# Six split-weight places instead of four, one product order for all paired projections, and seven-product gqk, gv and gr in a hybrid decoder layer

## The chip, the cores and the metric

The kernel runs on one core of one Trainium2 chip, in one launch. The metric is the device time of one execution in microseconds; lower is better. Nothing is shared between cores: there are no collectives. All inputs lie in HBM as float32, already cut by the host into tiles of 128 rows by 512 columns.

## The reference

One decoder layer on 256 tokens of width 2048, all in float32. The tokens are normalised and multiplied by one wide combined projection. Its slices feed three mixers, whose outputs are projected back, gated, added and projected once more. A gated feed-forward network follows.

```
h = rmsnorm(x, attn_norm)
proj = h @ w_in
(gq, gk, gv, gr, ga1, sq, sk, sv, mq, gates) = split(proj)
log_a = log_sigmoid(ga1 @ gla_w_a2 + gla_b_a) / 16
o_gla = rmsnorm(gla_mixer(gq, gk, gv, log_a)) ; y_gla = (o_gla * silu(gr)) @ w_br_gla
y_sb  = stick_breaking_mixer(rmsnorm(sq), rmsnorm(sk), sv) @ w_br_sb
y_mem = memory_mixer(rmsnorm(mq), m_k, m_v) @ w_br_mem       # m_k, m_v from rmsnorm(mem) @ w_mem_kv
merged = g0 * y_gla + g1 * y_sb + g2 * y_mem                  # g = sigmoid(gates)
x = x + merged @ w_o
gate, up = split(rmsnorm(x, ffn_norm) @ w_gate_up)
x = x + (silu(gate) * up) @ w_down
```

Widths: gq and gk are 512 each, gv, gr, sq, sk, sv and mq 1024 each, the three gates 2048 each, the feed-forward inner width is 5632. The linear attention (gla) has four heads with a state of 128 by 256 that is carried over chunks of 64 tokens; stick-breaking attention has eight heads of 128; the memory attention has four heads of 256 over 256 memory tokens.

## The kernel before

**Split products.** TensorE works here on a rounded float32 type, so each operand is split into a high part (rounded by ScalarE, `ACT`) and a low part (the difference, by VectorE, `DVE`). Each product of a 128x128 activation block with a 128x512 weight block is three matmuls: high by high, high by low, low by high. Activations are split once and kept. Weights are split as they come from HBM: `split` (lines 134 to 141) casts on ACT (line 137) and subtracts on DVE (line 138), 128 by 1024 elements at a time, which is two blocks of the contraction.

**Two kinds of places.** A *raw place* holds four weight blocks as loaded (1 MB); `loads` (line 161) takes one from the list `free_raw`, and its `done` gives it back. A *split place* holds the high and low part of two blocks; `parts` (line 166) walks round the list `splits`. `widen` (line 90) adds places of both kinds. Up to line 956 there are three raw and four split places of the pool `ring1`. Between lines 608 and 696 two more raw places lie in `opool`, in whatever outputs of 128x8x256 do not use yet, and up to line 748 one more in `pre`. From line 956 on `ring2` adds three raw places and one split place, and in the feed-forward part `ring3` adds one split place.

**Plain product.** `gemm` (line 183) makes one output block of 512 columns for both halves of 128 tokens: 16 contraction blocks by 2 halves by 3 matmuls are 96 matmuls. `project` (line 475) calls it twice for a width of 1024.

**Seven products.** `sgemm` (line 216) makes a pair of column blocks (j = 0, 1) for both token halves (t = 0, 1). Over 2p contraction blocks it multiplies a two by two block matrix by seven products instead of eight (Strassen's scheme in Winograd's form); the other contraction blocks are done plainly by `rest`. The products are `p1` to `p3`, `q4`, `p5` to `p7`, named a, b, e, f, g, h, i in the order list at lines 354 to 362. Products take 3p matmuls each and one split place for two blocks; a `rest` step takes 12 matmuls and one split place. The activation sums (`sx`, `sm_`, `sf`, `sd`) are made in advance by `make_forms`. The weight sums are made in the raw places: 21 += 22 in g and 21 += 12 in h by DVE (line 263), 22 += 12 by an accumulating DMA from the POOL queue (line 325). The sum 11 += 21 is made by DVE before f, or, where `moved` is set, by a second accumulating DMA in `p2` (line 305). `put` copies the first product from a `tmp` tile into an output in PSUM (line 288), and the later ones by DVE (line 290). PSUM has four `acc` and four `tmp` tiles; an `sgemm` uses four and two.

**The order list.** There are four orders: `late` (the activation sums are still being made), `moved`, p equal to 4 without `moved`, and p equal to 2. The instructions pass through a scheduler that lays out each engine's stream ahead of time by priority and its own cost estimates, so neighbours can change places; each engine then runs its stream in order.

**Background work.** `step`, called after each split, advances one piece of work from the list `background`: attention chunks, transposes, norms. `flush` runs all that is left.

**Stages around the change.** Plain: memory keys and values and mq, until about 142 us. Seven products with p = 4 through `wide` (line 672): sq, sk, sv, until about 293 us; the memory attention is background of sq, and it splits its outputs into `o_mem` at once (line 670). Plain: gqk and gv (lines 744 and 745, until about 396 us) with stick-breaking attention as background, which splits its outputs into `o_sb` (line 739). Then `pre` is released, the narrow decay projection `w_ga` runs (lines 751 to 766), then gr, plain (lines 899 to 908), with its sigmoid made of exponentials and a logarithm. The linear attention `gla` (line 789) is background once the first block of gr is issued. Then the memory branch: four times a plain gate block and a plain branch block, until about 604 us. Then seven products for the gates of the other two branches (`w_gate`, line 968, p = 4, not `moved`), with plain branch products between; then `w_o` (line 998, p = 2; the first call `late`); then the feed-forward part from about 951 us: eleven `w_gate_up` calls (line 1029, the first p = 2 and `late`, ten p = 4 and `moved`), five `w_down` calls (line 1067, p = 4, not `moved`), and two plain blocks at the end.

## Time and profile before

| What | Value |
|---|---|
| Median of 3 runs | 1646.2 us (1645.76 to 1649.24) |
| Profiled execution, its own time | 1647.21 us |
| Profiled execution, its span | 1645.4 us |
| Granted TensorE clock, mean over the span | 0.999 |
| Busy: TensorE, VectorE, ScalarE, GpSimd | 99%, 78%, 60%, 3% |
| Instructions on TensorE | 7314 matmuls, 7314 weight loads |
| Bytes moved by DMA | 368.82 MB |

The span goes from the first to the last instruction; the profiled execution's own time is 1.8 us longer, and 1.0 us above the median of the runs. A matmul's row shows its whole passage through the array, about 0.39 us for 512 columns; matmuls follow each other much closer than that, so what one costs has to be read from the distance between starts. "Idle" in a row is the time in which the engine did nothing just before the instruction, and behind the arrow stands what ended the wait.

### The profile page before, as it was taken

The page shows a single profiled execution, that of the slowest core. Times are in us where ns is not written, and L with a number is a line of the kernel's source. Part 1 is how long each engine was busy: PE and PEld are TensorE (multiplying, and loading weights), DVE is VectorE, ACT ScalarE, POOL GpSimd, SP SyncE. Part 2 cuts the span into 40 slices and gives each one's busy share as a digit, 9 for nine tenths or more (in the row PEclk, how much of TensorE's full clock was granted, in tenths as well). Part 3 has the DMA queues.
Part 4 walks back from the last instruction along what each step waited for, and adds up shares of the span by engine and source line. Part 5 has one row for each costly group of instructions (what it writes and reads, how often), then busy time and mean ns, then how long its engine had stood idle before and what let it go on. Part 6 is the DMA issues. An engine that isn't in the chain of part 4 may idle for free.

```text
span 1645.4 us, 19330 instructions
## 1 busy us (share of the span) xinstructions
PE 1629.8 (99%) x7314; PEld 1334.9 (81%) x7314; DVE 1291.2 (78%) x1491; ACT 988.0 (60%) x1204; POOL 53.8 (3%) x70
## 2 busy tenths in 40 slices
PE   8999999999999999999999999999999999999998
PEld 6888787888877878888888888888888888888887
DVE  6857788764565667887897798988888998888994
ACT  7755666654644556556555666666666666666662
POOL 0000000000000000000000000000110000110000
PEclk9999999999999999999999999999999999999999
DMA  8784575544544467667556758686897686897692
GB/s 327 280 325 125 189 249 158 200 161 156 183 154 154 157 228 284 191 215 255 174 210 220 254 181 259 216 298 234 258 274 255 193 302 240 257 271 253 193 343 89
DMA packets 59406, 368.82 MB, mean 224 GB/s; under 512 B 6544, under 2 KB 11152, under 8 KB 16688
## 3 DMA queue, kind: packets, MB, share of 16 engines
q1 hardware_dynamic: 49968, 320.17, 53.4%
q0 software_dynamic: 8704, 46.67, 14.2%
q8 instruction: 57, 0.93, 0.2%
q10 hardware_dynamic: 640, 0.75, 0.1%
q14 instruction: 37, 0.30, 0.1%
HBM read 320.89 MB, written 8.39 MB: 200 GB/s over the span
## 4 chain that ended last, share of the span: by engine, by line
PE 96%; DVE 1%; DMA 1%; ACT 1%; issue 0%; ACTq 0%; DVEq 0%
PE acc L250 15%; PE acc L251 15%; PE acc L248 15%; PE acc L209 10%; PE acc L210 10%; PE acc L211 10%; PE tmp L250 5%; PE tmp L251 5%; PE tmp L248 5%; PE tmp L431 2%; DVE wl L138 1%; ACT wh L137 1%; DMA raw<-in_w_gate_up 1%; DMA raw<-in_w_mem_kv 0%; PE tmp L635 0%; PE tmp L863 0%
## 5 line engine op out<-in xcount | busy, mean ns | idle before, releaser
L138 DVE TENSOR_TENSOR wl<-raw,wh 128x1024 fp32r<-128x1024 f32 (+1 forms) x728 | 876.9, 1220 | 278.4 <-ACT wh L137 267.4
L137 ACT CAST wh<-raw 128x1024 fp32r<-128x1024 f32 (+1 forms) x728 | 753.9, 1051 | 536.1 <-PE acc L211 212.9
L251 PE MATMUL acc<-wh,hl 128*128 128x512 f32 x452 | 175.9, 389 | 0.0
L250 PE MATMUL acc<-wl,hh 128*128 128x512 f32 x452 | 175.9, 389 | 0.0
L248 PE MATMUL acc<-wh,hh 128*128 128x512 f32 x452 | 175.8, 390 | 0.0
L209 PE MATMUL acc<-wh,xTh 128*128 128x512 f32 x384 | 152.7, 398 | 0.0
L211 PE MATMUL acc<-wh,xTl 128*128 128x512 f32 x384 | 149.9, 390 | 0.0
L210 PE MATMUL acc<-wl,xTh 128*128 128x512 f32 x384 | 149.8, 390 | 0.0
L263 DVE TENSOR_TENSOR raw<-raw 128x1024 f32<-128x1024 f32 x115 | 139.7, 1221 | 4.5 <-DMA raw<-in_w_gate_up 3.0
L209 PE MATMUL acc<-wh,oh 128*128 128x512 f32 x320 | 125.2, 393 | 2.6 <-ACT wh L137 1.6
L210 PE MATMUL acc<-wl,oh 128*128 128x512 f32 x320 | 124.9, 390 | 1.1 <-DVE wl L138 1.1
L211 PE MATMUL acc<-wh,ol 128*128 128x512 f32 x320 | 124.8, 390 | 0.0
L248 PE MATMUL acc<-wh,xTh 128*128 128x512 f32 x280 | 110.1, 395 | 1.3 <-ACT wh L137 1.3
L250 PE MATMUL acc<-wl,xTh 128*128 128x512 f32 x280 | 109.7, 392 | 0.5 <-DVE wl L138 0.5
L251 PE MATMUL acc<-wh,xTl 128*128 128x512 f32 x280 | 109.4, 391 | 0.0
L250 PEld LDWEIGHTS acc<-wl,hh 128*128 128x128 f32 x452 | 84.9, 188 | 17.7
L248 PEld LDWEIGHTS acc<-wh,hh 128*128 128x128 f32 x452 | 84.7, 188 | 17.8 <-ACT wh L137 0.2
L251 PEld LDWEIGHTS acc<-wh,hl 128*128 128x128 f32 x452 | 84.8, 188 | 17.6
L248 PE MATMUL tmp<-wh,sh 128*128 128x512 f32 x222 | 89.4, 403 | 1.8 <-ACT wh L137 1.7
L250 PE MATMUL tmp<-wl,sh 128*128 128x512 f32 x222 | 87.3, 393 | 0.7 <-DVE wl L138 0.7
L251 PE MATMUL tmp<-wh,sl 128*128 128x512 f32 x222 | 87.6, 395 | 0.0
L209 PEld LDWEIGHTS acc<-wh,xTh 128*128 128x128 f32 x384 | 72.2, 188 | 16.4 <-issue 2.2
(297 smaller groups left out, 2497.1 us busy)
## 6 DMA issues: line engine op xcount, KB each, us to landing
raw<-in_w_gate_up SPq DMA_DIRECT2D x88, 1024.0 KB, 5.9
raw<-in_w_in SPq DMA_DIRECT2D x72, 1024.0 KB, 4.9
raw<-in_w_down SPq DMA_DIRECT2D x44, 1024.0 KB, 6.5
raw<-raw POOLq DMA_DIRECT2D x35, 1024.0 KB, 7.9
raw<-in_w_gate SPq DMA_DIRECT2D x32, 1024.0 KB, 4.9
raw<-in_w_o SPq DMA_DIRECT2D x16, 1024.0 KB, 5.0
raw<-in_w_mem_kv SPq DMA_DIRECT2D x15, 1024.0 KB, 5.4
raw<-in_w_br_mem SPq DMA_DIRECT2D x8, 1024.0 KB, 5.2
```

What stands on the lines that cost most here:

```text
L137: act.copy(hi, src)
L138: dve.tensor_tensor(lo, src, hi.bitcast(F32), op=ALU.subtract)
L209: pe.matmul(o[t][:], xh[:, s], wh[:, j], start=k == 0, stop=False)
L210: pe.matmul(o[t][:], xh[:, s], wl[:, j], start=False, stop=False)
L211: pe.matmul(o[t][:], xl[:, s], wh[:, j], start=False, stop=k == nk - 1)
L248: pe.matmul(dst[:], xh, wh, start=id(dst) not in begun, stop=False, skip_group_check=True)
L250: pe.matmul(dst[:], xh, wl, start=False, stop=False, skip_group_check=True)
L251: pe.matmul(dst[:], xl, wh, start=False, stop=last, skip_group_check=True)
L263: dve.tensor_tensor(x, x, y, op=ALU.add)
L431: pe.transpose(dst, src, ident)
```

## The change

The change has five parts.

- **Places.** The raw places in `opool` are given up. `opool` gets one tag `o` with four places of equal size; the outputs use them, and two entries of `splits` point to them, so weights are split into six places instead of four, from line 608 on. One entry is taken back after gr and the other when `ring2` opens. `ring2` gets two raw and two split places instead of three and one. So raw places go from six to four in mq, sq, sk and sv, stay at four in gqk and gv, are four instead of three in gr, and five instead of six from `w_gate` to the end; split places go from four to six up to gr, to five in the memory branch, and later from five to six, and from six to seven in the feed-forward part.
- **Outputs split late.** `o_mem` and `o_sb` are first kept whole as float32, copied by ACT alone, and split later by `split_later` as background work: `o_mem` just before the memory branch, `o_sb` at the start of `w_gate`.
- **One order.** All calls but the `late` ones use one order, in which two steps of `rest` come between a and g, p7 follows p6, and p2 follows p7. `moved` is the default, so `w_gate` and the second `w_o` call make 11 += 21 by DMA; `late` calls never do, and `w_down` still uses DVE.
- **gqk, gv and gr by seven products**: gqk and gv with p = 2, gr with p = 4.
- **Order of stages.** gr stands before `w_ga`, with nothing in the background; `gla` becomes background of the memory branch alone.

```diff
-        splits.extend([(pool, w)] * w)
+        splits.extend([(pool, None, w)] * w)
...
-        pool, n = splits[turn[0] % len(splits)]
+        pool, tag, n = splits[turn[0] % len(splits)]
+        if tag:
+            both = pool.tile([P, 2, IT], F32R, tag=tag, name="w", bufs=n)
+            return [both[:, i] for i in range(2)]
...
-    def sgemm(xs, forms, w, blks, p, row0=0, late=False, moved=False):
+    def sgemm(xs, forms, w, blks, p, row0=0, late=False, moved=True):
...
-            if moved:
+            if moved and not late:
                 nc.gpsimd.dma_start(q[11][0][:, :p], q[21][0][:, :p], accum_op=ALU.add)
...
-            prod(o[1, 0], single(0, 1), 11, last, *([] if moved else [(11, 21)]))
+            prod(o[1, 0], single(0, 1), 11, last, *([] if moved and not late else [(11, 21)]))
...
-        elif moved:
-            seq = [a, g, *r0[:2], h, *r0[2:], b, e, *r1[:2], i, *r1[2:3], f, *r1[3:]]
-        elif p == SP:
-            seq = [a, g, *r0[:2], h, *r0[2:], e, *r1[:2], i, b, *r1[2:3], f, *r1[3:]]
         else:
-            seq = [a, *l21, g, *r0[:2], h, *r0[2:], e, *l12, *r1[:1], i, *l22, b, *l11, *r1[1:3], f, *r1[3:]]
+            seq = [a, *l21, *r0[:2], g, *r0[2:], h, *l22, i, b, *l11, *r1[:2], e, *l12, *r1[2:3], f, *r1[3:]]
...
-        return [opool.tile([P, 8, T], F32R, tag=f"o{x}", name=f"o{x}") for x in "hl"]
+        return [opool.tile([P, 8, T], F32R, tag="o", name=f"o{x}", bufs=4) for x in "hl"]
...
-    free_raw.extend([(pre, "raw", 1), (opool, "oh", 2), (opool, "ol", 2)])
+    free_raw.append((pre, "raw", 1))
+    splits.extend([(opool, "o", 4)] * 2)
...
-    o_mem = outT()
+    def whole():
+        return opool.tile([P, 8, T], F32, tag="o", name="o", bufs=4)
+
+    def split_later(o):
+        high, low = outT()
+
+        def work():
+            for c in range(0, 8, 4):
+                split(high[:, c : c + 4], low[:, c : c + 4], o[:, c : c + 4])
+                yield
+
+        background.append(work())
+        return high, low
+
+    o_mem = whole()
...
-        split(*(x[:, 2 * h : 2 * h + 2].rearrange("p c t -> p (c t)") for x in o_mem), o[:])
+        act.copy(o_mem[:, 2 * h : 2 * h + 2].rearrange("p c t -> p (c t)"), o[:])
...
-    def wide(dst, c0):
-        for j, result in sgemm(xs, sx, w_in, (c0 // NB, c0 // NB + 1), SP, moved=True):
+    def wide(dst, c0, p=SP):
+        for j, result in sgemm(xs, sx, w_in, (c0 // NB, c0 // NB + 1), p):
...
-        split(o_sb[0][:, h], o_sb[1][:, h], o[:, :T])
+        act.copy(o_sb[:, h], o[:, :T])
...
-    project(gqk, xs, w_in, O_GQ, r_x)
-    project(gv, xs, w_in, O_GV, r_x)
+    wide(gqk, O_GQ, 2)
+    wide(gv, O_GV, 2)
+    flush()
+    sqT = None
+    gr = section("gr", "b")
+    for j, result in sgemm(xs, sx, w_in, (O_GR // NB, O_GR // NB + 1), SP):
+        for t in range(2):
+            sg, o = ra()[:], result(t)
+            sigmoid(sg, o, t, False)
+            v = gr[:, t, j * NB : (j + 1) * NB]
+            act.activation(v, o, AF.Copy, scale=r_x[:, t : t + 1])
+            dve.tensor_tensor(v, v, sg, op=ALU.mult)
+    splits.pop()
+    o_mem = split_later(o_mem)
...
-    for n in range(0, MIX, NB):
-        o = gemm(xs, w_in, O_GR + n)
-        if n == 0:
-            background.append(gla())
...
+    background.append(gla())
...
-    widen("ring2", 3, 1)
+    splits.pop()
+    widen("ring2", 2, 2)
...
+    o_sb = split_later(o_sb)
     background.append(gla_T())
...
-            for j, result in sgemm(hs, sf, a["w_gate_up"], (i, NF + i), 4 if i else 2, late=i == 0, moved=i > 0):
+            for j, result in sgemm(hs, sf, a["w_gate_up"], (i, NF + i), 4 if i else 2, late=i == 0):
...
-            for j, result in sgemm(fs, sd, a["w_down"], blks, 4, row0=4 * part[0]):
+            for j, result in sgemm(fs, sd, a["w_down"], blks, 4, row0=4 * part[0], moved=False):
```

26 lines of the change are left out of this document (9 added, 17 removed).

## The prediction

> **What bounds the kernel now.** I read the page's totals and chain first, then the waits of TensorE, then the windows of the stages that the change touches.
>
> ```profile
> span 1645.4 us, 19330 instructions
> PE 1629.8 (99%) x7314; PEld 1334.9 (81%) x7314; DVE 1291.2 (78%) x1491; ACT 988.0 (60%) x1204; POOL 53.8 (3%) x70
> ...
> PE 96%; DVE 1%; DMA 1%; ACT 1%; issue 0%; ACTq 0%; DVEq 0%
> ...
> L209 PE MATMUL acc<-wh,xTh 128*128 128x512 f32 x384 | 152.7, 398 | 0.0
> ```
>
> TensorE is busy 99% of the span and holds 96% of the chain. So the time falls by the matmuls that go away and by what is left of its idle time, 1645.4 - 1629.8 = 15.6 us, which includes the start and the end. Its price per matmul is not the 398 ns of the group's row but the distance of starts. In a stretch without waits:
>
> ```profile
> 1195.75 0.39 PE L251 MATMUL acc<-wh,fl 128*128 128x512 f32 x1
> ...
> 1199.15 0.39 PE L251 MATMUL acc<-wh,fl 128*128 128x512 f32 x1
> ```
>
> Between these two starts lie 15 steps (five times three lines): 3.40 / 15 = **0.2267 us** per matmul of 512 columns.
>
> The windows of the stages (columns: the stretch, its length, then busy time and instructions of PE, PEld, DVE, ACT and POOL, the granted clock, the DMA share, GB/s):
>
> ```profile
> 146.00:205.00 59.00, 57.60 (x268) 46.95 (x267) 44.84 (x73) 36.81 (x59) 1.71 (x2) 1.00 0.51 167
> ...
> 248.00:293.00 45.00, 43.36 (x190) 34.90 (x189) 37.05 (x48) 29.82 (x35) 1.71 (x2) 0.96 0.63 187
> 293.00:400.00 107.00, 107.00 (x515) 90.02 (x514) 66.36 (x91) 62.34 (x92) 0.00 (x0) 1.00 0.47 160
> ...
> 445.00:604.00 159.00, 159.00 (x701) 124.74 (x700) 92.75 (x134) 75.39 (x104) 0.53 (x1) 1.00 0.49 166
> 604.00:755.00 151.00, 148.38 (x658) 121.56 (x657) 123.75 (x123) 87.83 (x98) 2.61 (x3) 1.00 0.69 231
> ...
> 997.00:1170.00 173.00, 173.00 (x779) 142.71 (x778) 157.38 (x158) 113.54 (x129) 9.56 (x11) 1.00 0.77 245
> ```
>
> TensorE is idle 1.40 us in sq, 1.64 us at the seam of sk and sv (with a clock of 0.96), and 2.62 us at the start of `w_gate`; in gqk, gv, the memory branch and the feed-forward part it is never idle, though DVE there goes up to 157.38 / 173 = 91%.
>
> **The change part by part.**
>
> *Matmuls removed.* Two plain blocks are 2 x 96 = 192 matmuls. With p = 4 a pair takes 7 products x 12 = 84, and 8 `rest` steps x 12 = 96: 180. With p = 2 it takes 7 x 6 = 42 and 12 x 12 = 144: 186. gqk and gv save 6 each, gr saves 12: 24 x 0.2267 = **-5.4 us**. The 384 high products of the quoted group become 192. Nothing else on TensorE is added.
>
> *What that adds beside it.* Splits grow from 16 to 19 in gqk and in gv and to 22 in gr. The prices:
>
> ```profile
> L138 DVE TENSOR_TENSOR wl<-raw,wh 128x1024 fp32r<-128x1024 f32 (+1 forms) x728 | 876.9, 1220 | 278.4 <-ACT wh L137 267.4
> L137 ACT CAST wh<-raw 128x1024 fp32r<-128x1024 f32 (+1 forms) x728 | 753.9, 1051 | 536.1 <-PE acc L211 212.9 <-PE acc L251 197.0 <-DVE raw L263 52.4
> ...
> L263 DVE TENSOR_TENSOR raw<-raw 128x1024 f32<-128x1024 f32 x115 | 139.7, 1221 | 4.5 <-DMA raw<-in_w_gate_up 3.0
> ...
> L380 DVE TENSOR_TENSOR cv<-acc,cv 128x512 f32<-128x512 f32 x48 | 32.6, 684 | 0.1
> ```
>
> In gqk and gv DVE gets 6 splits (7.3 us), 4 sums (4.9 us) and 10 `put` and result additions of 0.69 (6.9 us), and loses 8 low parts of `o_sb`, half as wide as the 684 ns row (an estimate of 0.34 each, 2.7 us): 66.4 + 16.4 = 83 us beside about 104 us of TensorE, 80%. gr has 22 splits, 4 sums and 5 additions, 35.2 us beside 180 x 0.2267 = 40.8, 86%. ACT gets 12 more casts of 1.05 us over stages where it is at 62.34 / 107 = 58%. All this is hidden by TensorE; without that cover it would be the 16.4 us in gqk and gv. `gla` loses gr as its cover and keeps the memory branch, where DVE is at 92.75 / 159 = 58% and where the code has 48 background steps for its 34: nothing.
>
> *The seam of sk and sv.* Here the first product a of sv is followed at once by g, with two sums and two splits for 12 matmuls, while DVE also reduces squares for the norm of sk:
>
> ```profile
> 250.05 0.39 PE L251 MATMUL tmp<-wh,sl 128*128 128x512 f32 x1
> 251.45 0.50 PE L248 MATMUL tmp<-wh,sh 128*128 128x512 f32 x1 [1.01 <-ACT wh L137]
> 252.39 0.73 PE L248 MATMUL acc<-wh,xTh 128*128 128x512 f32 x2 [0.45 <-ACT wh L137]
> 253.31 0.80 PE L250 MATMUL tmp<-wl,sh 128*128 128x512 f32 x1 [0.18 <-DVE wl L138]
> ...
> 256.97 0.40 PE L250 MATMUL acc<-wl,xTh 128*128 128x512 f32 x1
> ...
> 253.10:256.60 3.50, 3.32 (x9) 2.62 (x9) 3.50 (x7) 1.73 (x3) 0.00 (x0) 0.51 0.93 187
> ...
> L263 DVE TENSOR_TENSOR raw<-raw 128x1024 f32<-128x1024 f32 x4 | 4.9, 1221 | 0.0
> L487 DVE TENSOR_REDUCE hn_ss<-ra 128x4 f32<-128x512 f32 x3 | 2.0, 680 | 0.0
> ```
>
> From 250.05 to 256.97 us are 13 starts, which would take 2.95 us and took 6.92: **4.0 us lost**, partly waiting and partly because the clock was at 0.51 for 3.5 us after it. In the new order two `rest` steps stand between a and g: 24 matmuls, 5.4 us, for two splits (2.4 us of DVE), and two more split places let ACT and DVE work further ahead. That is more than the waits, 1.01 + 0.45 + 0.18. I take -4.0, with 0 as the other end. (The Trainium skill, "TensorE: Matmul & The Clock Gate", Part 1, says that the clock falls back after an idle window of about 3.4 us. Here it fell after gaps of at most 1.4 us between starts, so the row decides; by that rule the halved clock would have had no cause in the waits, and the term would be the waits alone, -1.6 us.)
>
> *The other two idle places.*
>
> ```profile
> PE acc L248 <- ACT wh L137: 0.9, 1, 0.9
> PE acc L250 <- DVE wl L138: 0.5, 1, 0.5
> ...
> ACT oh L140 <- PE tmp L431: 5.8, 1, 5.8
> ```
>
> The first two are the waits of sq, behind the memory attention's softmax; two more places are 2.7 us of work ahead and would cover them, if ACT gets to them: -0.7, from -1.4 to 0. The third is from the start of `w_gate`. There ACT stood 5.8 us behind a split of `gla_T` that waited for a transpose, and the casts behind it came late. Now `split_later` of `o_sb` comes before `gla_T`, two casts of 1.05 us and two differences of 1.22, and g comes 5.4 us later. I take half of the 2.62 us, -1.3, and from -2.6 to +2.6.
>
> *What may get worse.* A `rest` step right behind a needs the copy of the first product in its output for t = 0. In the second `w_o` call it stands so already:
>
> ```profile
> 908.42 0.57 ACT L288 COPY acc<-tmp 128x512 f32<-128x512 f32 x1
> ...
> 908.53 0.48 PE L248 MATMUL acc<-wh,oh 128*128 128x512 f32 x1
> ```
>
> The step's matmuls start before the copy has ended, so the scheduler puts the six of t = 1 first; their 1.36 us cover the 0.57: 0. Without that cover it would be up to 0.57 us in each of some 25 calls.
>
> The tail of gr: its four blocks of sigmoid now leave within one `rest` step of each other, and the flush adds the split of `o_mem`.
>
> ```profile
> L775 ACT ACTIVATE sg<-acc,nr_x 128x512 f32<-128x512 f32 x2 | 1.4, 682 | 0.3 <-PE acc L211 0.3
> L907 ACT ACTIVATE gr<-acc,r_x 128x512 f32<-128x512 f32 x2 | 1.4, 680 | 0.0
> L777 ACT ACTIVATE sg<-sg 128x512 f32<-128x512 f32 x2 | 1.3, 630 | 0.1
> L778 ACT ACTIVATE sg<-sg 128x512 f32<-128x512 f32 x2 | 1.3, 627 | 0.0
> ...
> 396.00:402.00 6.00, 6.00 (x50) 5.94 (x49) 2.46 (x3) 2.81 (x4) 0.00 (x0) 1.00 0.50 175
> ```
>
> ACT needs 4 x 2.62 + 2 x 1.05 = 12.6 us; the last `rest` (2.7) and `w_ga` (6.0 us, the window) cover 8.7. Behind ACT's chain stand the casts of the memory branch, and TensorE waits for those. Uncovered are 3.9 us unless places were filled before. Five places at 2.7 us would do it, so I take +1.0, from 0 to +3.9.
>
> Raw places: with four instead of six, the place of 21 is freed only when its accumulation has landed, and SP's loads queue behind it.
>
> ```profile
> SPq L242 <- DMA raw<-raw: 57.4, 12, 10.0
> ...
> ACT wh L137 <- PE acc L251: 28.0, 30, 1.7
> ...
> raw<-in_w_in SPq DMA_DIRECT2D x72, 1024.0 KB, 4.9
> ...
> DMA to landing us min/median/max: 5.6/7.4/13.9
> ```
>
> The order holds at most four raw places at once, so it fits, with loads of 4.9 us just in time. ACT waits today for a free split place (28.0 us in the feed-forward window), not for loads, so work is ahead. A p = 4 call has 40.8 - 35.2 = 5.6 us of DVE to spare, more than the mean wait of 57.4 / 12 = 4.8 and 4.4 less than the longest, 10.0: +0.5, from 0 to +4.4. The feed-forward part loses one of six raw places and gains one split place: 0.
>
> New accumulations: 22 += 12 by POOL for gqk, gv and gr, and 11 += 21 there, in `w_gate` and in the second `w_o` call, 11 more issues. POOL is 3% busy; behind them on its queue stand only the next accumulation and `w_o`'s stores. Product i now follows h directly: its casts are behind g's second split, two `rest` splits, and h's sums and splits, 7 x 1.22 = 8.5 us of DVE after the accumulation can start, against a median landing of 7.4 us: 0. `w_gate` loses 8 sums on DVE, hidden as well.
>
> **Sum**: -5.4 - 4.0 - 0.7 - 1.3 + 1.0 + 0.5 = **-9.9 us**. Against the profiled execution, 1647.2 with a span of 1645.4, that is 1637.3 and 1635.5. This execution lies 1.0 us above the median of the runs, 1646.2, from which I predict **1636.3 us**. The ends add up to -13.4 (1632.8) and +5.5 (1651.7).
>
> **Rivals.**
>
> *The stall moves.* h, i and b now stand in a row: 8 sums and splits and three `put`s, 9.8 + 2.1 = 11.9 us of DVE for 8.2 of TensorE. Where a norm falls beside them, a stall like that of 250 us comes back with its halved clock. For it: DVE's 37.05 of 45 us there. Against it: the two `rest` steps ahead leave 3.0 us (5.4 less 2.4), and there are two places more. It gives -9.9 + 4.0 = 1640.3.
>
> *The gain is eaten.* The tail of gr and the raw places cost their upper ends, +2.9 and +3.9 more: 1643.1, not to be told from no change (0.2% is 3.3 us, about what a measurement here can tell). For it: the twelve waits of SP's queue on accumulations. Against it: no wait of TensorE on a load is in the trace.
>
> *Slower: accumulations come late.* Product i decides at a landing of 8.5 us plus DVE's spare time, 9% of 40.8 or 3.7: over 12.2 us. If the landings were like the longest, 13.9, each of the fifteen new-order calls in the feed-forward part would lose 1.7 us: -9.9 + 25.5, or 1661.8. For it: DMA is at 0.77 there and one raw place is gone, so 12 is loaded later. Against it: the median, 7.4.
>
> ```profile
> L325 POOL DMA_DIRECT2D raw<-raw x25: 853/865/1019, 141.0 to 1577.8; - x25
> ```
>
> (The Trainium skill, "SBUF — State Buffer", in "SBUF: two separate sides", warns that a DMA issued by GpSimd can wait for its descriptors while a DVE instruction holds the ports that the two share. In this trace the issue took 853 to 1019 ns beside a DVE that is 78% busy, so no such blocking is seen; by that rule this rival would be the likeliest.)
>
> *It doesn't do what it says.* The places don't help because ACT stalls in order behind a transpose or a softmax, not for want of places. Then the 0.7 and 1.3 stay: 1638.3, within the forecast's range.
>
> **Chances.** Forecast, 1633 to 1640, with the last rival in it: 0.58. Moved stall: 0.20. Eaten: 0.12. Late accumulations: 0.10. Below 1642.9 lie 0.57 of the forecast and 0.15 of the moved stall: faster by over 0.2%, 0.72. Within 0.2% lie the rest of these two but 0.01, and 0.12 of the eaten gain: 0.17. Slower: 0.11. The range, **1632.5 to 1648**, leaves out the late accumulations and a little at both ends; above 1648 the bounds of the unknown costs go on to 1651.7, with little chance.
>
> **What would show it.** Right: the high products of the plain group fall to 192 and TensorE's instructions to 7290; no halved clock between 200 and 300 us; its idle time in that stretch under 0.5 us; L325 28 times. Wrong: idle time of TensorE before line 762 or the first gate block (tail of gr), ACT waiting for `raw<-in_w_in` (raw places), or for `raw<-raw` in the feed-forward part (accumulations), where TensorE's idle time is 0 now.

## The result, and the profile after

The changed kernel takes **1668.8 us** (median of 4 runs, 1667.2 to 1671.5) where the kernel before, run beside it on the same chip, takes 1646.0 (1645.2 to 1649.2). The ratio is 1.0136, with a 95% interval of 1.0118 to 1.0155: slower by 22.8 us. The forecast was 1636.3 us with a range of 1632.5 to 1648. The profiled execution took 1668.8 us, with a span of 1667.0.

The totals of the page after, and its chain of waits by engine and by line (lines from 212 on stand three higher than before, so that 209 became 212, and 325 became 328):

```profile
span 1667.0 us, 19308 instructions
PE 1637.7 (98%) x7290; PEld 1331.3 (80%) x7290; DVE 1304.9 (78%) x1506; ACT 1007.1 (60%) x1229; POOL 62.9 (4%) x81
...
PE 72%; DVE 13%; DMA 11%; issue 2%; ACT 2%; ACTq 0%; DVEq 0%; SPq 0%; POOLq 0%
PE acc L251 12%; PE acc L254 11%; PE acc L253 11%; PE acc L212 8%; PE acc L213 8%; PE acc L214 8%; DVE wl L138 7%; DMA raw<-raw 5%; PE tmp L251 4%; PE tmp L253 3%; PE tmp L254 3%; DMA raw<-in_w_in 3%; DMA raw<-in_w_gate_up 2%; ACT wh L137 1%; DVE raw L266 1%
```

24 matmuls are gone, and yet TensorE's share of the chain fell from 96% to 72%: 13% now go through DVE and 11% through DMAs, 5% through the accumulating ones (`raw<-raw`). TensorE's idle time is 1667.0 - 1637.7 = 29.3 us, nearly twice the 15.6 before.

The waits after, all engines, with those of the casts on transfers (columns: engine, tile and line, what it waited for, us in total, times, longest), then the waits of SP's queue:

```profile
ACT wh L137 <- DMA raw<-raw: 45.0, 16, 7.1
...
ACT wh L137 <- DMA raw<-in_w_gate_up: 12.0, 7, 4.7
...
ACT wh L137 <- DMA raw<-in_w_in: 11.6, 5, 2.8
...
ACT w L137 <- DMA raw<-in_w_in: 5.9, 6, 1.9
```

```profile
SPq L245 <- DMA raw<-raw: 137.2, 35, 14.5
...
SPq L200 <- DMA raw<-raw: 33.9, 5, 15.0
```

Before, the first of these rows was:

```profile
ACT wh L137 <- DMA raw<-raw: 6.5, 3, 2.7
```

Where the time came from shows in the windows by stage, cut at the first matmul of each stage (`w_gate` and `w_o`; the feed-forward part; its last `w_down` call and the end). In the changed kernel 19 matmuls of a plain pair stand ahead of product a of the feed-forward part, so that part begins at 956.1 us, and not with product a at 960.5. Columns as in the prediction's windows. Before:

```profile
604.80:951.10 346.30, 343.68 (x1542) 283.15 (x1540) 281.34 (x288) 201.76 (x233) 7.98 (x11) 1.00 0.67 226
951.10:1577.10 626.00, 625.21 (x2803) 516.27 (x2802) 560.90 (x576) 406.18 (x462) 38.40 (x46) 1.00 0.79 250
1577.10:1645.40 68.30, 64.06 (x285) 52.26 (x284) 45.89 (x50) 28.01 (x31) 0.88 (x1) 1.00 0.49 174
```

After:

```profile
606.90:956.10 349.20, 346.36 (x1540) 284.67 (x1541) 274.22 (x284) 202.33 (x235) 12.31 (x16) 0.99 0.70 232
956.10:1591.60 635.50, 630.57 (x2803) 515.16 (x2802) 557.97 (x574) 408.31 (x462) 38.47 (x47) 1.00 0.79 248
1591.60:1667.00 75.40, 67.10 (x285) 53.68 (x283) 44.63 (x49) 26.72 (x29) 0.43 (x1) 0.95 0.47 160
```

In the last call 285 matmuls took 68.3 us before and 75.4 after, with the clock at 0.95. Over the whole span, measured at the same first matmuls (us):

| stage | before | after | difference |
|---|---|---|---|
| start to sq | 142.1 | 141.8 | -0.3 |
| sq to `w_gate` | 462.6 | 465.2 | +2.6 |
| `w_gate` to the feed-forward part | 346.3 | 349.1 | +2.8 |
| feed-forward part to its last call | 626.2 | 635.5 | +9.3 |
| last call to the end | 68.3 | 75.4 | +7.1 |

The largest part lies in the feed-forward part ahead of its last call, where both kernels run 2803 matmuls and TensorE is idle for 4.9 us instead of 0.8. There the casts wait nine times for an accumulation, eight of them for the one that b starts (26.6 us), and seven times for a load of `w_gate_up` (12.0 us).

The last call shows the mechanism in one place. From the timelines after, POOL, then ACT, then TensorE (start, duration, instruction, and in brackets the idle time before it and what ended it):

```profile
1583.76 1.10 POOL L1067 DMA_DIRECT2D x2s<-x2d  x2 [12.19 <-PE acc L254]
1591.15 0.88 POOL L328 DMA_DIRECT2D raw<-raw  x1 [6.29 <-DVE cv L379]
```

```profile
1596.61 2.01 ACT L137 CAST wh<-raw 128x1024 fp32r<-128x1024 f32 x2
1605.70 3.89 ACT L137 CAST wh<-raw 128x1024 fp32r<-128x1024 f32 x4 [7.08 <-DMA raw<-raw]
```

```profile
1606.42 0.39 PE L254 MATMUL tmp<-wh,sd 128*128 128x512 f32 x1
1607.75 0.50 PE L251 MATMUL acc<-wh,fh 128*128 128x512 f32 x1 [0.94 <-ACT wh L137]
1611.09 0.80 PE L253 MATMUL acc<-wl,fh 128*128 128x512 f32 x1 [2.84 <-DVE wl L138]
```

The accumulation in h is issued at 1591.15 us and lands 14.47 later. ACT comes to i's cast at 1605.70 - 7.08 = 1598.6, that is 7.5 us after the issue, and stands there for 7.08 us. ACT runs its stream in order, so the casts of the steps behind i, whose weights had long landed, stand there with it, and DVE's low parts with them. TensorE lives off the split places that are filled, until 1606.4, and then starves; when the accumulation has landed, ACT and DVE must first make up for what they had not done. Then the clock is halved, as it is at the start of `w_gate`. The two stretches:

```profile
609.30:616.10 6.80, 5.42 (x13) 4.28 (x14) 5.52 (x7) 0.32 (x1) 0.69 (x1) 0.50 0.44 154
1609.40:1616.20 6.80, 4.88 (x11) 3.42 (x12) 6.80 (x8) 3.51 (x5) 0.00 (x0) 0.50 0.46 154
```

In them 13 and 11 matmuls start, 0.43 us apart where nothing waits (1612.11 and 1612.54 us, for example) instead of 0.23. So the halved clock costs some 2.6 and 2.2 us besides the waits, an estimate from these numbers. The second stretch begins 1.15 us into the wait of 2.84 us. (The Trainium skill, "TensorE: Matmul & The Clock Gate", Part 1, puts the fall behind an idle window of about 3.4 us. Here shorter waits were enough, so the rows decide.)

The start of `w_gate` has another cause. Counted from its first matmul, the changed kernel is 1.8 us behind after 100 matmuls of 512 columns (30.4 us for 28.6). DVE's timeline after:

```profile
605.33 0.69 DVE L951 TENSOR_TENSOR merged<-acc,sg 128x512 f32<-128x512 f32 x1 [4.16 <-PE acc L214]
606.53 1.22 DVE L138 TENSOR_TENSOR ol<-o,oh 128x1024 fp32r<-128x1024 f32 x1 [0.51 <-PE acc L213]
...
608.28 1.22 DVE L138 TENSOR_TENSOR ol<-o,oh 128x1024 fp32r<-128x1024 f32 x1
609.41 2.35 DVE L138 TENSOR_TENSOR wl<-raw,wh 128x1024 fp32r<-128x1024 f32 x2
```

The late split of `o_sb` (`ol<-o,oh`) and the last `merged` sums stand ahead of the first low part of `w_gate`, and DVE is idle for 4.16 us just before them, for it waits for the branch's outputs. TensorE waits for that low part, as the waits from 605 to 616 us have it:

```profile
PE tmp L253 <- DVE wl L138: 2.8, 1, 2.8
```

The late split alone does not make this stall: in a later version that keeps it (gr with two chunks, 1652.0 us), DVE makes two low parts of `w_gate` ahead of it, at 602.4 and 605.1 us, and TensorE does not wait here.

The third kind of loss is a place that comes free late. In the first call of sq an accumulation was issued at 163.50 us and landed 7.34 us later, at 170.85. SP's next loads stand behind it and go out at that moment; then ACT's cast waits for the load, and TensorE for the cast (timelines after of SP, ACT and TensorE):

```profile
170.86 0.94 SPq L245 DMA_DIRECT2D raw<-in_w_in  x2
...
175.84 1.04 ACT L137 CAST wh<-raw 128x1024 fp32r<-128x1024 f32 x1 [2.54 <-DMA raw<-in_w_in]
```

```profile
178.37 0.73 PE L251 MATMUL acc<-w,xTh 128*128 128x512 f32 x2 [2.29 <-ACT w L137]
```

Behind this wait, from 179.2 us, the granted clock is 0.50 for 3.41 us.

### The profile page after: what moved, and what is told of

The parts are those of the page before. It is cut to its first block, busy times and chain, and to the rows that moved or that the text cites. A ratio compares the mean times of both kernels' runs of the same rounds, so it can differ in the third digit from the quotient of the medians.

```text
span 1667.0 us, 19308 instructions
## 1 busy us (share of the span) xinstructions
PE 1637.7 (98%) x7290; PEld 1331.3 (80%) x7290; DVE 1304.9 (78%) x1506; ACT 1007.1 (60%) x1229; POOL 62.9 (4%) x81
## 3 DMA queue, kind: packets, MB, share of 16 engines
q0 software_dynamic: 10288, 55.58, 17.2%
## 4 chain that ended last, share of the span: by engine, by line
PE 72%; DVE 13%; DMA 11%; issue 2%; ACT 2%; ACTq 0%; DVEq 0%; SPq 0%; POOLq 0%
PE acc L251 12%; PE acc L254 11%; PE acc L253 11%; PE acc L212 8%; PE acc L213 8%; PE acc L214 8%; DVE wl L138 7%; DMA raw<-raw 5%; PE tmp L251 4%; PE tmp L253 3%; PE tmp L254 3%; DMA raw<-in_w_in 3%; DMA raw<-in_w_gate_up 2%; ACT wh L137 1%; DVE raw L266 1%
## 5 line engine op out<-in xcount | busy, mean ns | idle before, releaser
L138 DVE TENSOR_TENSOR wl<-raw,wh 128x1024 fp32r<-128x1024 f32 (+1 forms) x682 | 818.7, 1220 | 253.6 <-ACT wh L137 245.5
L137 ACT CAST wh<-raw 128x1024 fp32r<-128x1024 f32 (+1 forms) x682 | 706.4, 1050 | 469.1 <-PE acc L254 169.0
L251 PE MATMUL acc<-wh,xTh 128*128 128x512 f32 x334 | 133.2, 399 | 1.8 <-ACT acc L291 1.8
L254 PE MATMUL acc<-wh,xTl 128*128 128x512 f32 x334 | 130.5, 391 | 0.0
L253 PE MATMUL acc<-wl,xTh 128*128 128x512 f32 x334 | 130.5, 391 | 0.0
L213 PE MATMUL acc<-wl,oh 128*128 128x512 f32 x308 | 120.3, 391 | 1.1 <-DVE wl L138 1.1
L138 DVE TENSOR_TENSOR w<-raw,w 128x1024 fp32r<-128x1024 f32 x58 | 70.7, 1222 | 21.5 <-ACT w L137 21.1
L137 ACT CAST w<-raw 128x1024 fp32r<-128x1024 f32 x58 | 60.5, 1050 | 39.5 <-PE acc L254 13.4
L251 PEld LDWEIGHTS acc<-wh,xTh 128*128 128x128 f32 x334 | 62.9, 188 | 16.0 <-ACT acc L291 3.8
L253 PE MATMUL acc<-wl,fh 128*128 128x512 f32 x184 | 72.6, 394 | 2.8 <-DVE wl L138 2.8
```

The costliest lines, as they stand in the source:

```text
L137: act.copy(hi, src)
L138: dve.tensor_tensor(lo, src, hi.bitcast(F32), op=ALU.subtract)
L213: pe.matmul(o[t][:], xh[:, s], wl[:, j], start=False, stop=False)
L251: pe.matmul(dst[:], xh, wh, start=id(dst) not in begun, stop=False, skip_group_check=True)
L253: pe.matmul(dst[:], xh, wl, start=False, stop=False, skip_group_check=True)
L254: pe.matmul(dst[:], xl, wh, start=False, stop=last, skip_group_check=True)
```

## The experiments

A run's median stands beside the median of the kernel before in the same comparison; intervals are 95%.

### The three parts, one at a time

*Seven products for gqk, gv and gr alone.* Old places, old orders, `w_gate` and `w_o` without the second accumulation, gr at p = 4 before `w_ga`:

```diff
-    project(gqk, xs, w_in, O_GQ, r_x)
-    project(gv, xs, w_in, O_GV, r_x)
+    wide(gqk, O_GQ, 2)
+    wide(gv, O_GV, 2)
...
-        o = gemm(xs, w_in, O_GR + n)
+    for j, result in sgemm(xs, sx, w_in, (O_GR // NB, O_GR // NB + 1), SP):
```

> The kernel before with only gqk, gv and gr by seven products (and gr moved ahead of w_ga); places, orders and accumulations as before. If the lost time comes from the places or from the order, this one gains the 24 matmuls, 24 x 0.2267 = 5.4 us: about 1640.5 us, with TensorE's idle time as before, some 16 us. If the seven products of gqk, gv and gr bring the stalls themselves, it is slower than before, by up to the 22.8 us.

Measured: 1653.2 us beside 1646.3, ratio 1.0043 (1.0028 to 1.0058). With 24 matmuls fewer it is slower. The loss lies in gr, whose four-chunk call in the old order runs with the four raw places that are left there. The window of gr, and the waits in it:

```profile
400.00:440.00 40.00, 31.68 (x116) 24.08 (x115) 18.09 (x18) 16.11 (x20) 0.86 (x1) 0.87 0.62 194
```

```profile
ACT wh L137 <- DMA raw<-in_w_in: 15.7, 3, 6.9
```

TensorE is idle for 8.3 of 40 us there, and the clock is 0.87.

*The order alone.* Old places, old products; the one order for all but `late` calls, and `moved` as the default:

```diff
-        elif moved:
-            seq = [a, g, *r0[:2], h, *r0[2:], b, e, *r1[:2], i, *r1[2:3], f, *r1[3:]]
...
+        else:
+            seq = [a, *l21, *r0[:2], g, *r0[2:], h, *l22, i, b, *l11, *r1[:2], e, *l12, *r1[2:3], f, *r1[3:]]
```

> The kernel before with only the one order (and the default that makes 11 += 21 by the POOL queue in w_gate and the second w_o call); places and plain gqk, gv, gr as before. If the order is the cause (product i right behind h waits for the accumulation into 22), it is slower by 15 to 25 us, and ScalarE's casts wait some 45 us for accumulations, as in the changed kernel, against 6.5 before. If the raw places are the cause, it is within 3 us of before, or faster by the 4 us of the stall at the seam of sk and sv.

Measured: 1668.7 us beside 1646.3, ratio 1.0135 (1.0118 to 1.0152): by itself the whole loss of the change. All of it lies from `w_gate` on: to the feed-forward part 354.4 us for 346.3, then 634.8 for 626.2, then 75.9 for 68.3. The waits of its first `w_gate` call (612 to 634 us):

```profile
DVE wl L138 <- ACT wh L137: 9.4, 2, 8.1
ACT wh L137 <- DMA raw<-raw: 8.0, 1, 8.0
...
PE acc L251 <- ACT wh L137: 3.9, 1, 3.9
```

The landing there took 12.6 us. One wait of 8.0 us on ACT becomes 8.1 on DVE and 3.9 on TensorE.

*The places and the late splitting alone.* Old orders, old products:

```diff
-    free_raw.extend([(pre, "raw", 1), (opool, "oh", 2), (opool, "ol", 2)])
+    free_raw.append((pre, "raw", 1))
+    splits.extend([(opool, "o", 4)] * 2)
...
-    widen("ring2", 3, 1)
+    widen("ring2", 2, 2)
```

> The kernel before with only the places changed (six split places and four raw places up to gr, five raw and one more split place later, outputs split late); orders and plain gqk, gv, gr as before. If the raw places are the cause, it is slower by 15 to 25 us, with casts waiting for loads. If the order is the cause, within 3 us of before.

Measured: 1675.8 us beside 1646.3, ratio 1.0176 (1.0157 to 1.0195). 17.6 us of it lie between sq and `w_gate` (480.2 for 462.6). The three parts alone lose 6.9 + 22.4 + 29.5 = 58.8 us, together 22.8: they aren't additive.

*The order and the products, with the old places and outputs split at once.* The changed kernel with:

```diff
-    free_raw.append((pre, "raw", 1))
-    splits.extend([(opool, "o", 4)] * 2)
+    free_raw.extend([(pre, "raw", 1), (opool, "oh", 2), (opool, "ol", 2)])
...
-        act.copy(o_mem[:, 2 * h : 2 * h + 2].rearrange("p c t -> p (c t)"), o[:])
+        split(*(x[:, 2 * h : 2 * h + 2].rearrange("p c t -> p (c t)") for x in o_mem), o[:])
...
-    widen("ring2", 2, 2)
+    widen("ring2", 3, 1)
```

> The changed kernel with the places of before (six raw places in sq, sk, sv, six from w_gate on, outputs split at once). If the raw places are the cause, alone or by what they do to the new order, nearly all comes back: about 1640 us. If the order is the cause whatever the places, it stays near 1668 us.

Measured: 1672.3 us beside 1646.3, ratio 1.0160 (1.0144 to 1.0175). So under the new order the new places are worth a gain of 3.5 us, while under the old order they cost 29.5. The added split place helps most where the new order hurts: the feed-forward part with its last call takes 714.2 us here and 710.9 in the changed kernel.

### Raw places

The kernel before without the two raw places in `opool`, and nothing in their stead:

```diff
-    free_raw.extend([(pre, "raw", 1), (opool, "oh", 2), (opool, "ol", 2)])
+    free_raw.extend([(pre, "raw", 1)])
```

> The kernel before with the two raw places of opool left out, and nothing in their stead: four raw and four split places in mq, sq, sk and sv. If the loss of the places in that stretch (from the first product of sq to w_gate 480.4 us against 462.7) is the want of raw places under the old order, this kernel loses at least as much there: 15 to 25 us, about 1665 us. If it is the late splitting of the outputs or the sharing of their places with weights, it is within 3 us of before.

Measured: 1682.0 us beside 1646.5, ratio 1.0223 (1.0207 to 1.0238). So it is the raw places that cost, not the late splitting or the shared room. The waits, and the window of sq to sv:

```profile
ACT wh L137 <- DMA raw<-in_w_in: 37.7, 11, 7.7
```

```profile
142.10:293.00 150.90, 132.32 (x570) 105.49 (x570) 106.91 (x158) 84.02 (x117) 4.45 (x5) 0.93 0.51 154
```

TensorE is idle for 18.6 of 150.9 us, and the clock is 0.93. The wait is the one that the prediction named as the sign of short raw places; before it was 2.6 us in all. By the order list, places 21, 22 and 12 are held in the old order when b asks for the fourth, so that the loads of the plain pairs go out only when one of these comes free.

### The distance from an accumulation to its reader

The order alone again, but i after b and two plain pairs:

```diff
-            seq = [..., h, *l22, i, b, *l11, *r1[:2], e, *l12, *r1[2:3], f, *r1[3:]]
+            seq = [..., h, *l22, b, *l11, *r1[:2], i, e, *l12, *r1[2:3], f, *r1[3:]]
```

> The kernel before with the one order, but with product i (p7) put two rest steps after b (p2) instead of right behind h (p6), so that i again comes well after the accumulation into 22 starts and f comes one product later after b. If the loss of the one order comes from i and f standing too close behind their accumulations, most of its 22.4 us goes: at most 3 us over before, perhaps 4 us under it, and ScalarE's casts wait under 15 us for accumulations instead of 44.4. If it comes from the two rest steps between a and g, or from the 11 += 21 made by the POOL queue in w_gate, it stays near 1668 us.

Measured: 1646.5 us beside 1646.5, ratio 1.0004 (0.9995 to 1.0013): the order's whole loss is gone. The accumulations land no sooner: the first one in `w_gate` takes 13.15 us here and 12.63 in the order alone. Only nobody stands in front of them any more; the whole of the waits, and the feed-forward part:

```profile
ACT wh L137 <- DMA raw<-raw: 2.4, 2, 1.5
```

```profile
951.00:1576.00 625.00, 625.00 (x2788) 513.91 (x2786) 555.92 (x571) 406.40 (x457) 37.03 (x44) 1.00 0.80 251
```

This edit moves two readers at once: i away from the accumulation in h, and f, since i now stands between b and f, away from the one in b. In the order alone, 12 of the 15 waits were on the accumulation of b (27.3 us) and 3 on that of h (17.2 us). Two runs part them.

*f one plain pair later, at the end of a call.*

```diff
-            seq = [..., i, b, *l11, *r1[:2], e, *l12, *r1[2:3], f, *r1[3:]]
+            seq = [..., i, b, *l11, *r1[:2], e, *l12, *r1[2:], f]
```

> The order alone (1668.65 us), with product f one plain pair later, at the very end of a call; i stays right behind h and its plain pairs. f reads the sum that the accumulation in b makes, and 12 of the 15 waits of the casts for raw<-raw were on that one (27.3 of 44.4 us). Theory (both products stand too close, f costs the middle of the FFN, i costs the start of w_gate and the last part): the waits on the accumulation of b fall to under 5 us, the FFN up to its last part goes from 634.8 to about 628 us, w_gate to the FFN stays at about 354 and the last part at about 76; median 1661 (1658 to 1664). Rival A (i alone costs the time, f's waits are hidden by full split places): no change, 1666 to 1670. Rival B (f alone): 1650 or less.

With f last, column block 1 of a pair is finished ahead of block 0, so the feed-forward part multiplies a block by the gate of the call before, and the two blocks of `w_gate` change places; matmuls, splits and transfers are the same in number, but the output is not the layer's, and the run serves for its time alone. Measured: 1664.8 us beside 1646.3, ratio 1.0106 (1.0088 to 1.0125); its four times lie far apart, from 1661.8 to 1668.4, and the profile is of the longest. The waits on b's accumulation fell from 27.3 us to 7.4, those on h's stayed (19.8), and 3.9 us came back, half of what the first theory gave f. `w_gate` and the last call kept their loss (354.4 and 74.8 us).

*Two plain pairs from between g and h to between h and i.*

```diff
-            seq = [..., g, *r0[2:], h, *l22, i, b, ...]
+            seq = [..., g, h, *l22, *r0[2:], i, b, ...]
```

> The order alone (1668.65 us), with two plain pairs moved from between g and h to between h and i, so that i stands 5.4 us of TensorE later behind the accumulation in h, and f is where it was. Theory: w_gate to the FFN goes from 354.4 to about 347 us and the last part from 75.9 to about 69, the FFN between stays at about 635, the casts' waits on the accumulation of h go from 17.2 to under 3 us; median 1655 (1651 to 1659). Rival A (i alone): 1648 or less. Rival B (h, now right behind g, meets a new stall of its sums): the waits on the accumulation go as said, but the median stays above 1662, with TensorE waiting for h's splits in the FFN.

Measured: 1663.0 us beside 1646.3, ratio 1.0100 (1.0085 to 1.0115), 8 us above the theory. The feed-forward part up to its last call came back from 634.8 to 629.0 us, but the first call of `w_gate` and the last call did not: 351.9 and 76.5. There 5.4 us of TensorE between h and i are not enough. The waits of the first `w_gate` call (612 to 634 us):

```profile
ACT wh L137 <- DMA raw<-raw: 6.3, 1, 6.3
```

ACT still comes to i's cast 6.3 us early. It runs ahead of TensorE by as many steps as there are split places, so a distance counted in TensorE's time is shorter for ACT. Both expectations took the two distances as separate terms with a wait each; the two single steps give 3.9 + 5.7, the late i gives 22.2. Only more distance at both readers takes the long waits away.

*The loads of the residual in the last call.* In the order alone, two 1 MB loads (`x2s`) were issued on POOL's queue 8 us ahead of the late accumulation. This run moves their issue behind the first pair of columns:

```diff
-            for t in range(2):
-                nc.gpsimd.dma_start(x2s[t][:], x2d[:, t])
...
+            if not x2s:
+                for t, x in enumerate("hl"):
+                    x2s.append(fpool.tile([P, D], F32, tag=f"s{x}", name="x2s"))
+                    nc.gpsimd.dma_start(x2s[t][:], x2d[:, t])
```

> The kernel before with the one order, but with the two 1 MB loads of x2s issued on the POOL queue when the first pair of the last w_down call is done instead of just before it. If they are what makes the last accumulation into 22 land late (14.9 us), the last stage (75.9 us from the first w_down product of the last part to the end, 68.3 before) comes back to about 69 us, and the kernel takes about 1662 us. If the accumulation is late without them, nothing changes. The two loads may come late for the stores: up to 5 us the other way.

Measured: 1666.5 us beside 1646.5, ratio 1.0123 (1.0106 to 1.0139). It decides nothing: the loads had already waited for TensorE to free their tiles, and went out at the same place in the stream, 82.9 us ahead of the end against 83.8. The accumulation still took 14.2 us, and the last call 75.0. What part of that landing is due to the loads was not shown.

### Two chunks for gr

Seven products for the three alone, as in the first run, but gr at p = 2 too, in the old order of p = 2:

```diff
-    for j, result in sgemm(xs, sx, w_in, (O_GR // NB, O_GR // NB + 1), SP):
+    for j, result in sgemm(xs, sx, w_in, (O_GR // NB, O_GR // NB + 1), 2, moved=False):
```

> The kernel before with gqk, gv and gr by seven products, all three with p = 2 in the old order for p = 2 (rest steps between the products), places as before. gr then saves 6 matmuls instead of 12: 18 x 0.2267 = 4.1 us in all. If what ate the gain of the seven products was gr with p = 4 in four raw places, this gains about 4 us, 1642 us or less. If seven products in four raw places stall whatever p is, it is slower than before, as 1653.2 us was.

Measured: 1643.9 us beside 1646.5, ratio 0.9987 (0.9977 to 0.9996). 18 matmuls fewer are 4.1 us, and 2.7 of them arrive. The window in which the four-chunk call lost 8.3 us has no idle time:

```profile
400.00:440.00 40.00, 40.00 (x193) 33.73 (x191) 26.22 (x27) 24.36 (x31) 0.00 (x0) 1.00 0.59 207
```

### Mending the changed kernel step by step

*The late i where five raw places are free*, from `w_gate` on (the late i holds a fifth place, and the attention calls and groups have four):

```diff
+        elif len(free_raw) > 4:
+            seq = [a, *l21, *r0[:2], g, *r0[2:], h, *l22, b, *l11, *r1[:2], i, e, *l12, *r1[2:3], f, *r1[3:]]
         else:
```

> The changed kernel whole, but from w_gate on, where five raw places are free, product i stands after b and two plain pairs instead of right behind h and its plain pair. The attention calls and the groups keep the changed order, as they have four raw places. Theory (i waits there for an accumulation that lands after 12 us or more): w_gate to w_o falls from 260.7 to about 258 us, w_o to the FFN from 92.9 to 88.4, the FFN to the end from 706.6 to about 696, the casts' waits for raw<-raw from 45 to below 12 us in all, and the median from 1668.8 to 1651 (1648 to 1655); what is left over before sits ahead of w_gate. Rival (fewer raw places from w_gate on, five for six, cost the FFN its time): the time stays above 1662, with casts waiting for in_w_gate_up, because an i that stands later holds a place longer.

Measured: 1658.8 us beside 1645.6, ratio 1.0082 (1.0068 to 1.0095): 10 us come back, not 18. The last call is mended (69.6 us for 75.4), but the feed-forward part ahead of it keeps 6.7 of its 9.3 us. (The 92.9 us that the expectation has from `w_o` to the feed-forward part are cut at product a; to the first matmul they are 88.5, and 88.2 in the kernel before, so that little was to be gained there.) With five places instead of six the waits move to the loads:

```profile
ACT wh L137 <- DMA raw<-in_w_gate_up: 48.0, 16, 7.7
```

That was 12.0 us in the changed kernel. And the start of `w_gate`, with DVE's late split of `o_sb`, keeps its loss.

*In addition gqk, gv and gr in the old order of p = 2, gr with two chunks.*

```diff
+        elif p == 2 and not moved:
+            seq = [a, *l21, g, *r0[:2], h, *r0[2:], e, *l12, *r1[:1], i, *l22, b, *l11, *r1[1:3], f, *r1[3:]]
...
-    for j, result in sgemm(xs, sx, w_in, (O_GR // NB, O_GR // NB + 1), SP):
+    for j, result in sgemm(xs, sx, w_in, (O_GR // NB, O_GR // NB + 1), 2, moved=False):
```

> As the run with the late i from w_gate on; in addition gqk, gv and gr take products of two chunks, gr too, in the order that w_o's calls had before the change. Theory (in the groups it is the order, with too few raw places for four chunks, that loses, not the number of products): sq to w_gate falls from 465.1 us to about 459, as in the kernel before with the three projections at two chunks each (458.5), and the median is 5 to 6 us below the run with the late i alone, about 1645.5 (1643 to 1648), so that the change without its two faults is level with the kernel before or a little faster. Rival (the places for split weights in the attention calls are the fault there): sq to w_gate stays above 463 us and the gain over the run with the late i alone is under 2 us.

Measured: 1652.0 us beside 1645.6, ratio 1.0042 (1.0027 to 1.0057). The gain of 6.8 us is not where either theory put it: sq to `w_gate` stays at 464.5, and `w_gate` to the feed-forward part falls from 347.9 to 343.2, for the stall at its start is gone, though the late split of `o_sb` is still there. Why another order in gr removes that stall, two stages later, stays open.

*The old places besides*, which gives six raw places in the attention calls, and so the late i there too:

```diff
-    free_raw.append((pre, "raw", 1))
-    splits.extend([(opool, "o", 4)] * 2)
+    free_raw.extend([(pre, "raw", 1), (opool, "oh", 2), (opool, "ol", 2)])
...
-    widen("ring2", 2, 2)
+    widen("ring2", 3, 1)
```

> As the run with the late i and gr at two chunks (1652.0 us), with the old places besides: six raw places in the attention calls and from w_gate on, one place fewer for split weights, and the outputs split at once. As six places are free in the attention calls too, i stands late there as well. Theory (what that run still loses lies where a raw place is missing: 6.8 us ahead of w_gate and 5.2 us in the FFN against the kernel before with two-chunk projections and the late i in the attention calls alone): sq to w_gate falls from 464.5 to about 458 us, the FFN to the end from 701 to about 696, the casts' waits for in_w_gate_up from 31.7 to below 5 us, median 1642 (1640.5 to 1644.5). Rival (the places give as much as they take, and the rest is the order in the FFN): median 1648 or more.

Measured: **1642.7 us** beside 1646.1, ratio 0.9978 (0.9969 to 0.9987). It went as the theory had it: sq to `w_gate` 457.7, the feed-forward part with its last call 696.1, and these waits are all that is left of the casts on these transfers, with none on `in_w_gate_up`:

```profile
ACT wh L137 <- DMA raw<-in_w_in: 11.9, 6, 4.2
...
ACT wh L137 <- DMA raw<-raw: 2.4, 2, 1.4
```

*Both smaller distances in the changed kernel*, an order that fits four places (the order of outputs changes as with the late f above, and so this output is not the layer's either):

```diff
+            seq = [a, *l21, *r0[:2], g, h, *l22, *r0[2:], i, b, *l11, *r1[:2], e, *l12, *r1[2:], f]
```

> The changed kernel whole (1668.8 us), with both moves: two plain pairs from between g and h to between h and i, and f one plain pair later. It never needs a fifth raw place, so it fits the four and five of the changed kernel. Theory (the two distances are most of the loss, and the raw places then cost about 9 us, as the run with old places showed): w_gate to the FFN about 346, the FFN to the end about 700, sq to w_gate unchanged at 465; median 1653 (1649 to 1658), about the time of the run with the late i and gr at two chunks. Rival (with few raw places the waits only move to the loads): casts wait for in_w_gate_up or in_w_in instead, median above 1660.

Measured: 1662.6 us beside 1646.3, ratio 1.0098 (1.0083 to 1.0113). The rival holds. Its waits of the casts:

```profile
ACT wh L137 <- DMA raw<-raw: 32.6, 10, 6.7
...
ACT wh L137 <- DMA raw<-in_w_gate_up: 20.8, 15, 2.8
ACT w L137 <- DMA raw<-in_w_in: 20.7, 8, 6.8
```

### A version that beats both

The kernel before with gqk, gv and gr at two chunks, and the late i in the attention calls alone:

```diff
+        elif moved and p == SP and not ffn[0]:
+            seq = [a, *l21, *r0[:2], g, *r0[2:], h, *l22, b, *l11, *r1[:2], i, e, *l12, *r1[2:3], f, *r1[3:]]
         elif moved and p == SP:
```

> The kernel before with gqk, gv and gr by seven products of two chunks each (1643.85 us when it ran alone), and in the attention calls alone the order with i after b and two plain pairs; raw places as before. Theory (the new order is good where it leaves the accumulation over 8 products and six raw places are there): sq to w_gate loses another 1 to 2.5 us, because the stalls at 178 and 254 us shrink, median 1641.8 (1640.5 to 1643.5), ratio to before 0.997. Rival (the stall at the seam only moves, as with the order alone): no change to 1643.9, ratio 0.9985 to 0.9995.

Measured: **1642.6 us** beside 1645.6, ratio 0.9982 (0.9973 to 0.9991). It and the mended kernel with the old places, 1642.7, are level: 3.1 and 3.3 us under the kernel before. That the late i in the attention calls adds to the two-chunk products is likely by the medians (1643.9 to 1642.6), but the intervals overlap.

## Why the prediction was wrong

**New accumulations: 0.** This is the step that failed. The order alone is 22.4 us slower, and the late i, which moves f too, brings it all back; in the changed kernel it brings back 10.0 of the 22.8 us, as the waits then move to loads that lack a place. The step set 8.5 us of DVE "after the accumulation can start" against a median landing of 7.4. Both sizes were off where it matters. ACT came to i's cast 7.5 us after the issue in the last call, and 4.6 after it in the first call of `w_gate` of the order alone (issued at 615.1, reached at 627.7 - 8.0), since part of the counted splits was done before the issue. And the landings were 14.5 and 12.6 us. In the order alone these two rare ones stand behind most of the loss (8.1 us from `w_gate` to the feed-forward part, 7.6 in the last call); in the changed kernel the last call costs 7.1 of the 22.8 us. The prediction had a long landing in its own rows: the last accumulation of the kernel before took 13.9 us at the very place of the worst stall, and cost the cast no more than 1.5 us there, because i stood further behind.

It also looked at i alone. f in the new order stands nearer to b's accumulation, and in the changed kernel 12 of the waits (33.7 us) are on that one. Eight of them lie in the feed-forward part, which loses 9.3 us:

```profile
L308 POOL DMA_DIRECT2D raw<-raw x21: 851/858/897, 163.5 to 1570.7; - x21
...
  ACT wh L137: 33.7, 12
...
DMA to landing us min/median/max: 4.6/7.8/8.4
```

These landings are short, 7.8 us in the median, and still too long for the cover of five splits (two plain pairs, the two of e and one more pair, 5 x 1.22 = 6.1 us of DVE). In the `moved` order of before, and with the late i, seven stand there, 8.5 us. In the order alone, where the casts wait for no load in the feed-forward part and ten times for an accumulation (26.4 us), that part loses 8.6 us.

**The rival "accumulations come late"** had this mechanism and nearly the time, 1661.8 for 1668.8, and a chance of 0.10. That the time is near is luck. Its price, 1.7 us in fifteen calls or 25.5 us, all for i, was not how it came: the feed-forward part with its last call loses 16.4 us, by many short waits for f that places mostly cover, by loads, and by one long wait for i with a halved clock on top. What spoke against it, the median landing, was the wrong statistic for i, whose stream stops at its slowest transfer. Nothing shows the blocked descriptors by which the prediction would have called this rival the likeliest: the issues of the quoted row still take 851 to 897 ns. (The page of the Trainium skill that it cites, "SBUF — State Buffer", in "SBUF: two separate sides", ties them to DVE's two-port modes, and no run here shows DVE's mode.) What the trace shows beside a late one is other traffic. The accumulation of 12.6 us in the order alone is issued at 615.09 us, and up to 620.0 only the queue of the loads moves packets, and keeps the DMA engines 95% busy (queue, packets, MB, share of 16 engines):

```profile
q1 hardware_dynamic: 175, 1.30, 95.4%
```

**Raw places: +0.5, from 0 to +4.4.** Mis-sized. In the mended kernel the old places give back 9.3 us: 6.8 between sq and `w_gate`, together with the late i that they allow there, and 4.9 from the feed-forward part on, where the prediction put its **0** on one raw place fewer, with a loss of 1.7 between. Under the old order their lack costs 29.5 us with two split places in exchange (and the outputs split late) and 35.4 without. That the order "holds at most four raw places at once, so it fits" was true of the count and not of the time: a place whose accumulation is under way is held for the landing, and the next load waits behind it (SP's 137.2 us in 35 waits, quoted above, for 57.4 in 12).

**Seam of sk and sv: -4.0.** Too large, and in part luck. The seam's 40 matmuls of 512 columns, from 246.2 us on in the kernel before, take 13.1 us before, 10.9 in the changed kernel and 10.3 in the order alone: 2.8 were to be had. And 1.5 of these are the halved clock, which need not come: in the seven products alone, which keep order and places there, the same three waits stand (1.00, 0.45 and 0.18 us), the clock stays at 1.00, and the 40 take 11.6 us. Around the seam the changed kernel loses more than it gains. The windows of 200 to 300 us, before and after, and TensorE's waits in it after:

```profile
200.00:300.00 100.00, 98.36 (x440) 80.12 (x439) 83.69 (x109) 68.42 (x83) 3.42 (x4) 0.98 0.68 210
```

```profile
200.00:300.00 100.00, 94.63 (x429) 76.86 (x429) 80.25 (x104) 65.65 (x83) 3.41 (x4) 1.00 0.71 221
```

```profile
PE tmp L430 <- DVE sq L496: 2.2, 1, 2.2
PE acc L251 <- ACT acc L291: 1.8, 2, 1.5
PE tmp L430 <- DVE sk L496: 1.3, 1, 1.3
```

Idle 5.4 us for 1.6, with 429 matmul rows for 440. That is the rival "the stall moves": two of the waits are for the norms of sq and sk (line 496) that fall beside h, i and b. It takes the new places as well as the new order, for in the order alone no wait of TensorE there is over 0.85 us. With six raw places and the late i (the mended kernel), the first 552 matmuls of 512 columns from sq on take 151.8 us for 154.2. **The sq wait, -0.7**, became the wait of 2.29 us at 178 us with its halved clock, of which the quoted rows show the cause: a raw place.

**The copy behind a: 0.** Mis-sized by little. TensorE waits for that copy (line 291) three times in the changed kernel, 2.1 us in all, two of them in the rows above; the longest, 1.5, is more than the 0.57 us that the prediction had as its upper end.

**Start of `w_gate`: -1.3, up to +2.6.** Wrong in sign, within its bounds: +1.8 us after 100 matmuls, with the late split of `o_sb` on the path and 2.6 us of halved clock, which the term did not have, in it.

**Matmuls removed: -5.4.** Right in count (7290, and 140 + 52 = 192 high products in the plain group). In time, the two-chunk version shows 2.7 of its 4.1 us, and the two versions that have the late i besides 3.1 and 3.3.

**Tail of gr: +1.0.** Nothing of it shows: in the memory branch after (441.4 to 606.9 us) TensorE is busy for 165.25 of 165.5 us. The added splits on DVE and ACT were hidden, as said.

Of the signs that the prediction named, four of the right ones appeared (7290, 192, L328 28 times, no halved clock from 200 to 300 us), but not the idle time under 0.5 us there, and so did two of the wrong ones: casts waiting for `raw<-raw` in the feed-forward part, and for `raw<-in_w_in`.

## What to carry to other kernels

Ask of each transfer that is made within a call how far behind it the first instruction stands that needs it on the engine that runs ahead, not on the engine that sets the pace, and compare that with the longest landing in the trace of before, not with its median. An engine that runs in order and stops at one late operand stops all that is ready behind it, and more buffers between it and the engine that sets the pace cover only a part of the stop. A buffer that is both the target of an accumulation and the place for the next load counts for longer than its last reader, so whether an order fits is a matter of time, not of the number that are held.

## What the hardware showed besides

- Loads of 1 MB that are issued together land one after the other: four in the order alone, issued between 604.5 and 605.8 us, took 4.8, 6.9, 8.9 and 10.9 us, some 2.0 us for each that is ahead. An accumulating transfer of 1 MB from raw place to raw place took 7.9 us in the median of the changed kernel, one of 0.5 MB 4.7 us, and 12.6 to 14.9 us in places where several loads were under way beside it; in the last call of the changed kernel two loads in front of it on POOL's queue took 9.9 and 15.5 themselves. (The Trainium skill, "DMA: Bandwidth & Descriptors", in "SWDGE vs HWDGE vs iDMA", says that only GpSimd's queue can accumulate; in these traces all such transfers are issued there.)
- The granted clock fell to 0.50 for 3.4 to 10.2 us at a time. The waits ahead of it can be short: in the kernel before they were 1.01, 0.45 and 0.18 us within 3 us, and the same three left it at 1.00 in the seven products alone. The 3.41 us at 0.50 cost 1.5 us there (13.1 for 11.6). With the fewest raw places the clock was 0.990 in the mean over the span.
- The three parts of the change lose 6.9, 22.4 and 29.5 us alone and 22.8 together, so they interact: the new places cost under the old order and gain 3.5 us under the new one.
